# Two transformer blocks on one core: second-block attention with the values as stationary operand and strips turned two steps late; whole heads in the first block

## The chip, the cores and the metric

One core of a Trainium2 chip runs the whole program. The time is the device time of one execution in microseconds; what counts is the median over runs. TensorE (PE) multiplies, VectorE (DVE), ScalarE (ACT) and GpSimd (POOL) do elementwise work, and DMA queues issued by SyncE (SP) bring the weights.

## The reference

The input is 512 tokens of width 1024, in f32. Two blocks follow each other. In short:

```python
# block 1: proj = rmsnorm(x) @ w_in;  8 heads of width 64
logits = q @ k.T * scale + c_q - c_k          # c: cumulated log of a forget gate; causal
att = softmax(logits) @ v
sg  = u * (tril(w_s) @ rmsnorm(vg) + b_s)     # gated over chunks of 128 tokens, u, vg = gelu(...)
x  += concat(att, sg) @ w_out
x  += (silu(g) * a) @ w_down                  # a, g = split(conv3(rmsnorm(x) @ w_up)), 2816 wide
x   = rmsnorm(x)
# block 2: h = rmsnorm(x) * (1 + sc) + sh;  proj = h @ w_in_2
q, k, v = latent projections, rope on 32 of 96 columns     # "MLA", 8 heads, values 64 wide
o_mla = softmax(q @ k.T * scale, chunk-causal) @ v
o_ca  = softmax(cq @ ck.T * scale + rel_bias, chunk band) @ cv    # "chunk attention", 8 heads of 64
x += g_a * concat(o_mla, o_ca) @ w_out_2
x += g_m * conv_ffn(modulated rmsnorm(x))
```

## The kernel before

Activations lie as 128 partitions by columns. Large products are made exact enough by splitting both factors into a high and a low part and adding three products (hi by hi, hi by lo, lo by hi). `load_split` (L341 to L351) brings a weight by DMA into `wraw`, casts it to `whi` on ACT (L350) and subtracts to `wlo` on DVE or POOL (L351). The matrix product itself is one helper, so most TensorE rows carry its line, L372; the tiles' names tell them apart: `mm` are projections, `s` scores, `o` values.

TensorE takes its work in the order of the code. The other engines' work is ordered by a scheduler with priorities (`high_priority`), and each engine then works in order.

Both blocks' attention runs in `attention()` (L619 to L676), over a list of strips: a strip is 128 queries of one head against the `qi + 1` key blocks of 128 at or ahead of them (widths 128, 256, 384, 512). Step t does the following in this order:

- `strip_scores(t)`: the scores go into one bank of the pool `s` (three banks), DVE adds the bias or mask and keeps the minimum (L597), ACT takes the exponential into `p` and sums it (L601, with a read-accumulator instruction);
- background work `bg` (norms, rope), then half of the step's `fill` (projections and output products on TensorE, in amounts set by `rate(t)`);
- `strip_turn(t-1)`: the 128x128 blocks of `p` are transposed on TensorE (L610) back into the same `s` bank, which is copied to `pt` (L612) on whichever of ACT and DVE the scheduler chooses;
- the other half of `fill`, then `strip_values(t-2)`: per key block `pt` is the stationary operand (128x128) and `v` the moving one with 64 columns, f32; result `o` has queries on the partitions.

After the eight strips of a pair of heads, `pair_end` divides by the sums (L715, L717), transposes the result (L725) and splits it into `mix` for the output product. Heads prepare their operands in generators whose slices are taken ahead of need (`LEAD`, 5 steps). In block 1 `stack_k` casts and subtracts one half of `kh` and `kl` (L693, L694), and two DMAs on SP copy these to the other 64 partitions (L700).

In block 2 strips 0 to 31 (numbered within the block) are chunk attention, 32 to 63 are MLA. The q and k of a chunk-attention pair are transposed at L1633 after a norm (L1457); MLA's are transposed at L1667 and split into `hi`, `lo` (L1671 to L1675). Projections are evacuated from PSUM by `nc.any` (L1462, L1463, L1469, L1521, L1526, L1597). `final` (L942) scales the first block's result and is a background job; output part 0 needs it.

Of the kernel before, what the change touches and what calls it, by code (L numbers as in the profile page):

```python
# [19 lines left out]
P = 128  # L20
# [216 lines left out]
class Kernel:  # L237
# [99 lines left out]
    def load_split(self, src, pool, dest, skew):  # L337

        nc, n = self.nc, src.shape[-1]
        raw = self.wraw.tile([P, 1024], F32, tag="wraw", name="wraw")  # L340
        nc.sync.dma_start(out=raw[:, :n], in_=src)  # L341
        if dest:
            hi, lo = (self.pools[dest[0]].tile([P, 1024], F32R, tag=t, name="wsplit") for t in dest[1:])
        else:
            hi = self.whi.tile([P, 1088], F32R, tag="whi", name="whi")[:, skew:]
            lo = self.wlo.tile([P, 1088], F32R, tag="wlo", name="wlo")[:, skew:]
        with ExitStack() as ctx:
            for ins in self.before:
                ctx.enter_context(self.tc.issue_after(ins))
            nc.scalar.copy(hi[:, :n], raw[:, :n])  # L350
            (nc.gpsimd if pool else nc.vector).tensor_tensor(  # L351
                out=lo[:, :n], in0=raw[:, :n], in1=hi[:, :n].bitcast(F32), op=ALU.subtract)
        return hi, lo
# [264 lines left out]

    def attention(self, heads, fill, rate, bg, bgrate, mix, depth=1):  # L619

# [20 lines left out]
        for t in range(n + depth + 3):  # L641
            r = rate(t)
            if t < n:
                h, qi = seq[t]
                slices(h)
                sc[t] = self.strip_scores(hd[h], qi)
                for h in range(len(heads)):
# [5 lines left out]
            u = t - depth  # L653
            if 0 <= u < n:
                h, qi = seq[u]
                pt[u] = self.strip_turn(hd[h], qi, sc.pop(u))
            if t > n + depth:
                for f in later:
                    f()
                later = []  # L660
            fill.run(r / 2)
            for f in later:
                f()
            later = []
            u -= 1
            if 0 <= u < n:
                h, qi = seq[u]
                if u % 8 == 0:
                    o = self.bank("o")
                ov = 2 * qi + h % 2  # L670
                self.strip_values(hd[h], qi, pt.pop(u), o[:, ov * 64:(ov + 1) * 64])
                if h < last:
                    if u % 8 == 7:
                        later = [self.pair_end(o, mix, *hd[h]["end"])]
                elif u % 4 == 3:
                    later = [self.pair_end(o, mix, *hd[h]["end"], half=u % 8 // 4)]  # L676

# [11 lines left out]
    def stack_k(self, tiles, k, odd, scale=None):  # L689
        nc, (_, kh, kl) = self.nc, tiles  # L690
        a, b = HALF_P[::-1] if odd else HALF_P
        if scale is None:
            nc.scalar.copy(kh[a], k[a])  # L693
            nc.vector.tensor_tensor(out=kl[a], in0=k[a], in1=kh[a].bitcast(F32), op=ALU.subtract)  # L694
        else:
            nc.scalar.activation(out=kh[a], in_=k[a], func=AF.Copy, scale=scale[a])
            nc.vector.scalar_tensor_tensor(out=kl[a], in0=k[a], scalar=scale[a], in1=kh[a].bitcast(F32),
                                           op0=ALU.mult, op1=ALU.subtract)
        for t in (kh, kl):
# [9 lines left out]
    def pair_end(self, o, mix, sums, at, pool, tag, half=None):  # L709
# [12 lines left out]
        def turn():  # L722
# [6 lines left out]
            ins = self.split(mix[at], tp, c512)  # L729
            if half:  # L730

                self.before = ins
# [300 lines left out]
    def block1_mix(self, xn, x, evac, evac_last, norm_a):  # L1033
# [233 lines left out]
        def head(h):  # L1267
            fill.upto(f"qk{h // 2}") if h > 1 else None
            pr, odd = divmod(h, 2)
            sums, sh = self.sums(pairs, h)  # L1270

            cp = self.bank()
# [7 lines left out]
                in1=cmask.unsqueeze(1).to_broadcast([P, 4, P]), op=ALU.add)  # L1280
            yield
            tiles = self.stacked(stk)
            self.stack_q(tiles, qf[pr], odd)
            yield
            self.stack_k(tiles, kf[pr], odd)
            yield
            qs, kh, kl = tiles
# [8 lines left out]
            return dict(qk=[(qs, kh), (qs, kl)], bias=bias, v=lambda kb: vv[:, kb, h * 64:(h + 1) * 64], sums=sh,  # L1296
                        end=(sums, pr, mx, "mix"))

        cumulate()
        for _ in range(4):  # L1300
            fill.run(1500)
            bg.run(500)
        self.attention([head(h) for h in range(8)], fill, lambda t: 4500 if t < 0 else 3100, bg,
                       lambda t: 1300, mix)
        fill.drain()
# [55 lines left out]
    def block2_mix(self, xn, norm_b, final, evac, evac_last, norm_a):  # L1361
        nc, i = self.nc, self.i
        self.urgent = None
        ctx = ExitStack()
        self.pt = self.pool("pt2", 3, ctx=ctx)
        self.pp = self.pool("pp2", 3, ctx=ctx)
        self.att = self.pool("att2", 1, ctx=ctx)
        one = self.pools["one"] = self.pool("one2", 1, ctx=ctx)
        two = self.pool("two2", 2, ctx=ctx)
        stk = self.pool("stk2", 12, ctx=ctx)  # L1370
        tabq, tabk = tabs = [one.tile([P, 4, 4, 16], F32, name="tab" + z) for z in "qk"]
# [89 lines left out]
        def cq0_evac(t, ps):  # L1461
            nc.any.tensor_copy(out=ca_slice(t, 0, 0), in_=ps[:, 32:288])  # L1462
            nc.any.tensor_copy(out=kr[:, t], in_=ps[:, 0:32])  # L1463

        def ca_job(w, z, j, **kw):
            def dst(t):
                return vc[:, t, 256 * j:256 * (j + 1)] if z == 2 else ca_slice(t, z, j)

            yield from self.gemm_tm(i[w], 256, xn, lambda t, ps: nc.any.tensor_copy(out=dst(t), in_=ps), **kw)  # L1469
            if z < 2 and kw.get("pairs") != ((0, 1),):  # L1470
# [12 lines left out]
        def rope():  # L1483

            with self.tc.issue_after(self.applied):
                self.rope_tables(tabs)
            yield 6000

        def cq0():
            yield from self.gemm_tm(i["w_cq0"], 288, xn, cq0_evac)  # L1490
            bg.add("w_cq0", ca_norm(0, 0))
            bg.add("rope", rope())
            bg.add("final", final)

# [24 lines left out]
        def q_evac(c):  # L1519
            def f(t, ps):  # L1520
                nc.any.tensor_copy(out=mq[c][t // 2][:, t % 2], in_=ps.rearrange("p (h d) -> p h d", d=QK))  # L1521
            return f

        def k_evac(c):
            def f(t, ps):
                nc.any.tensor_copy(out=mk[c][t // 2][:, t % 2, :, 0:64],  # L1526
                                   in_=ps.rearrange("p (h d) -> p h d", d=64))
            return f
# [56 lines left out]
        def mla(c):  # L1585
            if c == 0:
                bg.add("kr", kr_rope())
            mq[c] = m_tiles(0, c)
            yield from self.gemm_tm(i[f"w_q{c}"], 384, [lath[0], lath[1]], q_evac(c))
# [6 lines left out]
            yield from self.gemm_tm(i[f"w_kv{c}"], 256, [lath[2]],  # L1596
                                    lambda t, ps: nc.any.tensor_copy(out=vm[c][:, t], in_=ps))  # L1597

# [57 lines left out]
        def mla_head(h):  # L1656
# [70 lines left out]
```

## Time and profile before

| what | us |
|---|---|
| median of 3 runs | 1227.69 (1226.39 to 1227.93) |
| profiled execution | 1225.62 |
| its span | 1223.9 |
| TensorE busy | 1193.0 |
| DVE busy | 780.2 |
| ACT busy | 526.5 |
| POOL busy | 190.5 |

The mean granted TensorE clock of the span is 0.997. TensorE's busy time is modelled at its ends, so a share of 97% doesn't say that it runs at its peak; what matters is where it sits idle, and which engine ends that. Block 1's mix stage lies at some 75 to 230 us, block 2's at some 575 to 880; the rest are the two feed-forward parts.

### The profile page before, as it was taken

The numbers are of one execution on the slowest core, as the hardware profiler recorded it, in microseconds if no ns is written. First come the engines' busy times: TensorE is split into PE (matmuls) and PEld (weight loads), VectorE is DVE, ScalarE is ACT, GpSimd is POOL, SyncE is SP. The second block draws the span as 40 slices with busy tenths as digits, with TensorE's granted clock in tenths as the row PEclk, the third lists the DMA queues.
The fourth block names the chain that finished last, engine by engine and source line by source line (L and its number), as shares of the span: only waits on it lengthen the run. The fifth ranks groups of instructions, "written<-read, shape, count | busy, mean of one in ns | idle before, by whom it ended". The sixth has DMA issues, their size and how long they took to land.

```text
span 1223.9 us, 17406 instructions
## 1 busy us (share of the span) xinstructions
PE 1193.0 (97%) x6730; PEld 1038.9 (85%) x6730; DVE 780.2 (64%) x1392; ACT 526.5 (43%) x946; POOL 190.5 (16%) x209
## 2 busy tenths in 40 slices
PE   9999898999999999999998989999999999999998
PEld 6898688988888888888998988899988888888887
DVE  6646777688888887433575878876675665653221
ACT  6535445454444443323434556655544444442110
POOL 2367301300000000000245472301200000000000
PEclk9999999999999999999999999999999999999999
DMA  7432222166666666433121333111133323233330
GB/s 237 120 102 78 82 82 61 53 188 196 200 192 190 193 190 190 144 98 128 58 86 57 87 109 104 36 36 36 53 123 102 103 86 104 93 89 112 114 110 18
DMA packets 42594, 135.78 MB, mean 111 GB/s; under 512 B 5120, under 2 KB 6016, under 8 KB 42512
## 3 DMA queue, kind: packets, MB, share of 16 engines
q1 hardware_dynamic: 34096, 106.84, 28.3%
q10 hardware_dynamic: 8208, 27.27, 7.4%
q8 instruction: 52, 0.85, 0.3%
q0 software_dynamic: 208, 0.57, 0.2%
q14 instruction: 30, 0.25, 0.1%
HBM read 128.37 MB, written 2.10 MB: 107 GB/s over the span
## 4 chain that ended last, share of the span: by engine, by line
PE 84%; DVE 6%; POOL 4%; issue 2%; ACT 2%; DMA 1%; SPq 0%; ACTq 0%; DVEq 0%; POOLq 0%
PE mm L372 74%; PE s L372 4%; PE o L372 3%; PE s L610 2%; POOL wlo L351 1%; ACT whi L350 1%; DVE wlo L351 1%; DVE s L597 1%; DVE ca L1457 1%; DMA x<-in_xT_dram 1%; POOL gelu L1111 0%; PE mm L1667 0%; DVE nt L557 0%; ACT p L601 0%; PE s L725 0%
## 5 line engine op out<-in xcount | busy, mean ns | idle before, releaser
L351 DVE TENSOR_TENSOR wlo<-wraw,whi 128x1024 fp32r<-128x1024 f32 (+4 forms) x182 | 210.3, 1157 | 180.6 <-ACT whi L350 179.5
L372 PE MATMUL mm<-xnh,whi 128*128 128x512 f32 (+1 forms) x832 | 310.8, 374 | 5.6 <-DVE x L877 2.7
L350 ACT CAST whi<-wraw 128x1024 fp32r<-128x1024 f32 (+4 forms) x194 | 191.6, 991 | 277.8 <-PE mm L372 260.2
L372 PE MATMUL mm<-xnl,whi 128*128 128x512 f32 (+1 forms) x832 | 309.7, 372 | 0.0
L372 PE MATMUL mm<-xnh,wlo 128*128 128x512 f32 (+1 forms) x832 | 309.7, 372 | 0.0
L372 PEld LDWEIGHTS mm<-xnh,whi 128*128 128x128 f32 x832 | 156.2, 188 | 33.5 <-DVE x L877 2.9
L372 PEld LDWEIGHTS mm<-xnh,wlo 128*128 128x128 f32 x832 | 156.1, 188 | 27.6
L372 PEld LDWEIGHTS mm<-xnl,whi 128*128 128x128 f32 x832 | 156.2, 188 | 26.7
L372 PE MATMUL mm<-gh,whi 128*128 128x512 f32 (+1 forms) x384 | 141.3, 368 | 1.1 <-DVE x L967 0.6
L372 PE MATMUL mm<-gh,wlo 128*128 128x512 f32 (+1 forms) x384 | 141.1, 367 | 0.0
L372 PE MATMUL mm<-gl,whi 128*128 128x512 f32 (+1 forms) x384 | 141.0, 367 | 0.0
L759 DVE SCALAR_TENSOR_TENSOR cv<-mm,cols,cv 128x510 f32<-128x510 f32 (+1 forms) x176 | 130.3, 745 | 2.5 <-ACT cv L757 0.5
L372 PE MATMUL mm<-whi,xnh 128*128 128x256 f32 (+3 forms) x304 | 96.5, 318 | 1.1 <-ACT xnh L842 1.1
L372 PE MATMUL mm<-wlo,xnh 128*128 128x256 f32 (+3 forms) x304 | 93.6, 308 | 0.2 <-DVE wlo L351 0.2
L372 PE MATMUL mm<-whi,xnl 128*128 128x256 f32 (+3 forms) x304 | 93.6, 308 | 0.1
L372 PEld LDWEIGHTS mm<-gh,whi 128*128 128x128 f32 x384 | 72.1, 188 | 13.5 <-DVE x L967 0.8
L372 PEld LDWEIGHTS mm<-gh,wlo 128*128 128x128 f32 x384 | 72.1, 188 | 12.1
L372 PEld LDWEIGHTS mm<-gl,whi 128*128 128x128 f32 x384 | 72.1, 188 | 12.0
L601 ACT ACTIVATE p<-s,st 128x128 f32<-128x128 f32 (+1 forms) x96 | 50.7, 528 | 70.4 <-DVE st L597 64.6
L1028 DVE CUSTOM_DVE_ANT_0 wada<-wada,cs,cols 128x1024 f32<-128x1024 f32 x48 | 61.5, 1282 | 28.9 <-DMA wada<-in_w_ada_dram 28.8
L372 PE MATMUL mm<-mix,whi 128*128 128x256 f32 (+1 forms) x288 | 73.8, 344 | 2.6 <-DVE x L877 1.5
L757 ACT ACTIVATE cv<-mm,cols 128x512 f32<-128x512 f32 x88 | 67.6, 773 | 0.0
(296 smaller groups left out, 1793.2 us busy)
## 6 DMA issues: line engine op xcount, KB each, us to landing
wraw<-in_w_up_dram SPq DMA_DIRECT2D x88, 512.0 KB, 3.6
wada<-in_w_ada_dram ACTq DMA_DIRECT2D x48, 512.0 KB, 3.7
wraw<-in_w_down_dram SPq DMA_DIRECT2D x32, 512.0 KB, 3.6
wraw<-in_w_out_dram SPq DMA_DIRECT2D x16, 512.0 KB, 3.7
wraw<-in_w_down_dram SPq DMA_DIRECT2D x16, 384.0 KB, 3.2
wraw<-in_w_qk_dram SPq DMA_DIRECT2D x8, 512.0 KB, 4.2
wraw<-in_w_v_dram SPq DMA_DIRECT2D x8, 256.0 KB, 4.9
x<-in_xT_dram SPq DMA_DIRECT2D x8, 256.0 KB, 6.5
```

Of the source, the lines that this page charges most:

```text
L350: nc.scalar.copy(hi[:, :n], raw[:, :n])
L351: (nc.gpsimd if pool else nc.vector).tensor_tensor(out=lo[:, :n], in0=raw[:, :n], in1=hi[:, :n].bitcast(F32), op=ALU.subtract)
L372: self.nc.tensor.matmul(out, lhsT, rhs, start=start, stop=stop, **kw)
L597: self.urgent = nc.vector.tensor_tensor_reduce(out=s[:, cs], in0=s[:, cs], in1=b, scale=1.0, scalar=3e38 if j == 0 else st[:, j - 1:j], op ...
L601: nc.scalar.activation(out=p[:, :nk], in_=s[:, :nk], func=AF.Exp, bias=st[:, len(parts) - 1:len(parts)], scale=-1.0, accum_out=hd["sums"](qi))
L610: self.nc.tensor.transpose(s[:, c], p[:, c], self.ident)
L757: nc.scalar.activation(out=t, in_=ps, func=AF.Identity, scale=w[2], bias=self.col(cb, n))
L759: nc.vector.scalar_tensor_tensor(out=t[:, d:], in0=ps[:, :512 - d], scalar=w[2 - d], in1=t[:, d:], op0=ALU.mult, op1=ALU.add)
L1028: nc.vector.tensor_tensor_reduce(out=w, in0=w, in1=self.cs, scale=1.0, scalar=self.col("b_ada_2", n), op0=ALU.mult, op1=ALU.add, accum_out ...
L1457: nc.vector.tensor_tensor(out=v3, in0=v3, op=ALU.mult, in1=ss[:, j, z, t].unsqueeze(2).to_broadcast([P, 4, 64]))
```

## The change

In block 2, `attention` is called with `depth=2, side=True`. A strip is now turned two steps behind its scores, by `side_turn` (transposes at L629, the copy always on ACT at L630 and into one tile for the head's four strips). After a pair's last strip `pair_values` multiplies for both heads with `v` (64 columns) as stationary operand and up to 512 columns of `pt` as moving one; the two heads alternate, one writing partitions 0 to 63 of `o`, the other 64 to 127. `side_end` no longer transposes `o` but the broadcast reciprocals of the sums (L793 on ACT, L799 on TensorE, L803 on ACT), and multiplies. There are four buffers for exponentials (`pp2`), two for turned heads, and nine for stacked operands. Evacuations go to ACT, `final` becomes a job of the second MLA part, and three pieces of fill (1500) with background work stand ahead of the loop. In block 1 a head is built in one piece two strips ahead (`ahead=2`) at high priority, and the second half of `kh` and `kl` is made by ACT and DVE in place of DMAs. POOL's share of `wlo` is cut in pieces of 256 columns.

```diff
@@ load_split
+            step = 256 if pool else n
+            for o in range(0, n, step):
+                c = slice(o, min(o + step, n))
+                (nc.gpsimd if pool else nc.vector).tensor_tensor(
+                    out=lo[:, c], in0=raw[:, c], in1=hi[:, c].bitcast(F32), op=ALU.subtract)
@@
+    def side_turn(self, pt, qi, sp):
+        nk = (qi + 1) * P
+        s, p = sp
+        for kb in range(qi + 1):
+            c = slice(kb * P, (kb + 1) * P)
+            self.nc.tensor.transpose(s[:, c], p[:, c], self.ident)
+        self.nc.scalar.copy(pt[:, qi:4 * qi + 1:3], s[:, :nk].rearrange("p (k q) -> p k q", q=P))
+
+    def pair_values(self, hds, pts, o, half=None):
+        q0, q1 = (0, 4) if half is None else (2 * half, 2 * half + 2)
+        for kb in range(q1):
+            a = max(q0, kb)
+            for z, (hd, pt) in enumerate(zip(hds, pts)):
+                p = pt.rearrange("p a b -> p (a b)")[:, (3 * kb + a) * P:(3 * kb + q1) * P]
+                self.mm(o[HALF_P[z], a * P:q1 * P], hd["v"](kb), p, kb == 0, kb == q1 - 1)
@@ attention, in step t
+            if ahead:
+                with self.tc.high_priority(offset=AHEAD):
+                    for h, _ in seq[:t + ahead + 1]:
+                        slices(h)
...
             fill.run(r / 2)
+            if side:
+                for f in later:
+                    f()
+                later = []
+                u = t - depth
+                w = u - 1
+                if 0 <= w < n and w % 8 == 7 or n - 8 <= w < n and w % 4 == 3:
...
+                    self.pair_values([hd[h - 1], hd[h]], [pt[h - 1], pt[h]], o, half)
+                    later = [self.side_end(o, mix, *hd[h]["end"], half=half)]
+                if 0 <= u < n:
...
+                    self.side_turn(pt[h], qi, sc.pop(u))
+                fill.run(r / 2)
@@ stack_k
         if scale is None:
-            nc.scalar.copy(kh[a], k[a])
-            nc.vector.tensor_tensor(out=kl[a], in0=k[a], in1=kh[a].bitcast(F32), op=ALU.subtract)
+            for o in (a, b):
+                nc.scalar.copy(kh[o], k[a])
+                nc.vector.tensor_tensor(out=kl[o], in0=k[a], in1=kh[a].bitcast(F32), op=ALU.subtract)
+            return
@@ side_end
+        nc.vector.reciprocal(sums[:, c8], sums[:, c8])
+        nc.scalar.copy(att[:, c512].rearrange("p (g d) -> p g d", d=64),
+                       sums[:, c8].unsqueeze(2).to_broadcast([P, 2 * len(qs), 64]))
+        def turn():
+            tp = self.bank()
...
+                nc.tensor.transpose(tp[:, t * P:(t + 1) * P], att[:, t * P:(t + 1) * P], self.ident)
...
+            nc.scalar.copy(att[:, c512], tp[:, c512])
+            nc.vector.tensor_tensor(out=att[:, c512], in0=o[:, c512], in1=att[:, c512], op=ALU.mult)
+            ins = self.split(mix[at], att, c512)
@@ block 2
-        self.pt = self.pool("pt2", 3, ctx=ctx)
-        self.pp = self.pool("pp2", 3, ctx=ctx)
+        self.pt = self.pool("pt2", 2, ctx=ctx)
+        self.pp = self.pool("pp2", 4, ctx=ctx)
-        stk = self.pool("stk2", 12, ctx=ctx)
+        stk = self.pool("stk2", 9, ctx=ctx)
-            nc.any.tensor_copy(out=ca_slice(t, 0, 0), in_=ps[:, 32:288])
+            nc.scalar.copy(ca_slice(t, 0, 0), ps[:, 32:288])
...
+        for _ in range(3):
+            fill.run(1500)
+            bg.run(800)
         self.attention(
             heads, fill,
-            lambda t: 3000 if t < 0 else 2000 if t < 16 else 1600 if t < 34 else 500,
-            bg, lambda t: 1700 if t < 16 else 600, mix)
+            lambda t: 1500 if t < 0 else 1900 if t < 16 else 1600 if t < 34 else 600,
+            bg, lambda t: 1700 if t < 34 else 1200, mix, depth=2, side=True)
```

On TensorE before, at two MLA strips in the second block (`s_7688` and `s_7715`; `s_7665` is the strip ahead of them), the order is scores, the turn of the strip ahead, projections, values:

```order
L372 MATMUL s_7688<-hi_7547,hi_7510 128x384 [waits PE_49]
L372 MATMUL s_7688<-lo_7548,hi_7510 128x384
L372 MATMUL s_7688<-hi_7547,lo_7511 128x384
L610 MATMUL s_7665<-ident_156,p_7671 128x128 [waits Activation_49]
L610 MATMUL s_7665<-ident_156,p_7671 128x128
L372 MATMUL mm_7701<-mix_7295,whi_7146 128x512 x2
L372 MATMUL mm_7701<-mix_7295,wlo_7147 128x512
L725 MATMUL s_7705<-ident_156,att_7686 128x128 [waits DVE_49]
L725 MATMUL s_7705<-ident_156,att_7686 128x128 x3
L372 MATMUL o_7713<-vm_6652,pt_7676 128x64 [waits PE_49]
L372 MATMUL s_7715<-hi_7547,hi_7510 128x512 [waits Activation_49]
```

On TensorE of the changed kernel at the same two strips (`s_7627`, then `s_7655`), with the values of a pair between them:

```order
L376 MATMUL mm_7636<-mix_7339,wlo_7126 128x512
L376 MATMUL o_7640<-pt_7465,vm_6595 64x512
L376 MATMUL o_7640<-pt_7559,vm_6595 64x512
L376 MATMUL o_7640<-pt_7465,vm_6595 64x384
L376 MATMUL o_7640<-pt_7559,vm_6595 64x384
L376 MATMUL o_7640<-pt_7465,vm_6595 64x256
L376 MATMUL o_7640<-pt_7559,vm_6595 64x256
L376 MATMUL o_7640<-pt_7465,vm_6595 64x128
L376 MATMUL o_7640<-pt_7559,vm_6595 64x128
L629 MATMUL s_7590<-ident_156,p_7596 128x128
L376 MATMUL s_7655<-hi_7522,hi_7482 128x512 [waits Activation_49]
```

The values moved from every step into one group per pair, and the turn is now that of the strip two steps back (`s_7590`), right ahead of the scores of the strip that uses its bank.

On ACT before, at the same place, exponentials (L601) and the copies of turned strips (L612); a copy follows the exponential of its own strip:

```order
L601 ACTIVATE p_7671,sums_7504<-s_7665,st_7669 128x256
L612 COPY pt_7698<-s_7665 128x256
L601 ACTIVATE p_7694,sums_7504<-s_7688,st_7692 128x384
L741 CAST mix_7710<-s_7705 128x512
L1671 CAST hi_7729<-mm_7724 96x512
L612 COPY pt_7736<-s_7688 128x384
L601 ACTIVATE p_7721,sums_7504<-s_7715,st_7719 128x512
```

On ACT of the changed kernel a few strips on (exponentials L605, copies L630):

```order
L605 ACTIVATE p_7695,sums_7476<-s_7689,st_7693 128x128
L630 COPY pt_7652<-s_7627 128x3x128
L605 ACTIVATE p_7727,sums_7476<-s_7721,st_7725 128x256
L630 COPY pt_7652<-s_7655 128x4x128
L605 ACTIVATE p_7743,sums_7476<-s_7737,st_7741 128x384
L630 COPY pt_7750<-s_7689 128x128
```

The copy of a strip (`s_7627`) now stands behind the exponential of the strip two later (`s_7689`), and the strip after that (`s_7721`) takes over its bank.

## Rows read from the trace of the kernel before

**Rows 1.** Page, part 1: busy time, share of the span, instructions.

```profile
PE 1193.0 (97%) x6730; PEld 1038.9 (85%) x6730; DVE 780.2 (64%) x1392; ACT 526.5 (43%) x946; POOL 190.5 (16%) x209
```

**Rows 2.** Windows: stretch, length; PE, PEld, DVE, ACT, POOL busy; clock; DMA share, GB/s.

```profile
659.30:662.70 3.40, 3.40 (x19) 3.40 (x18) 2.34 (x4) 1.80 (x4) 0.00 (x0) 0.50 0.11 33
664.40:767.10 102.70, 97.61 (x746) 92.75 (x744) 79.85 (x187) 58.49 (x148) 47.03 (x54) 1.00 0.33 92
767.10:832.00 64.90, 64.43 (x478) 59.26 (x478) 49.50 (x129) 40.34 (x109) 9.43 (x11) 1.00 0.10 34
```

**Rows 3.** Waits of TensorE, 570 to 890: total, times, longest.

```profile
PE mm L1633 <- DVE ca L1457: 3.4, 2, 2.2
PE mm L1633 <- DVE qs L687: 3.0, 2, 2.7
```

**Rows 4.** Waits of TensorE, 75 to 230.

```profile
PE mm L372 <- DVE mix L745: 2.8, 2, 2.6
PE mm L372 <- DVE kf L1186: 2.3, 1, 2.3
```

**Rows 5.** Timeline, TensorE, 654 to 665: start, length, instruction [idle before].

```profile
654.45 0.27 PE L1633 MATMUL mm<-ident,ca 128*128 128x128 f32 x1
...
658.45 1.21 PE L1633 MATMUL mm<-ident,ca 128*128 128x128 f32 x6 [2.17 <-DVE ca L1457]
659.31 0.56 PE L372 MATMUL mm<-whi,xnh 128*128 128x256 f32 x1
...
662.65 0.32 PE L372 MATMUL mm<-whi,xnh 128*128 128x256 f32 x1
...
664.42 0.28 PE L372 MATMUL s<-kh,qs 128*128 128x256 f32 x1
```

**Rows 6.** Timeline, MLA strips of the four widths, 783 to 794.

```profile
783.73 0.36 PE L372 MATMUL s<-hi 96*128 96x256 f32 x1
...
785.64 0.19 ACT L601 ACTIVATION_READ_ACCUMULATOR p<-s,st 128x1 f32 x1
...
786.32 0.36 PE L372 MATMUL s<-hi 96*128 96x256 f32 x1
...
787.58 1.00 PE L372 MATMUL o<-vm,pt 128*128 128x64 f32 x8
...
787.86 0.19 ACT L601 ACTIVATION_READ_ACCUMULATOR p<-s,st 128x1 f32 x1
788.38 0.42 PE L372 MATMUL s<-hi 96*128 96x384 f32 x1
...
789.47 0.37 ACT L612 COPY pt<-s 128x256 f32<-128x256 f32 x1 [1.42 <-PE s L610]
...
790.44 0.19 ACT L601 ACTIVATION_READ_ACCUMULATOR p<-s,st 128x1 f32 x1
790.50 0.47 PE L372 MATMUL s<-hi 96*128 96x512 f32 x1
...
792.40 0.36 PE L372 MATMUL s<-hi 96*128 96x256 f32 x1
...
793.35 0.20 ACT L601 ACTIVATION_READ_ACCUMULATOR p<-s,st 128x1 f32 x1
```

**Rows 7.** Source line L612, 575 to 878: ns min/median/max.

```profile
L612 ACT COPY pt<-s x51: 253/393/589, 669.1 to 835.4; 128x128 f32<-128x128 f32 x14, 128x512 f32<-128x512 f32 x14, 128x256 f32<-128x256 f32 x13, 128x384 f32<-128x384 f32 x10
```

**Rows 8.** Timeline, block 1: f32 products that stream 256 columns.

```profile
124.20 1.46 PE L372 MATMUL mm<-uv,wsp 128*128 128x256 f32 x6
...
125.49 0.49 PE L610 MATMUL s<-ident,p 128*128 128x128 f32 x3
```

**Rows 9.** Value records by form, chunk-attention and MLA stretch: busy, mean ns.

```profile
L372 PE MATMUL o<-vc,pt 128*128 128x64 f32 x146 | 19.6, 264 | 0.4 <-ACT pt L612 0.4
L372 PE MATMUL o<-vm,pt 128*128 128x64 f32 x138 | 18.6, 263 | 0.0
```

**Rows 10.** Block 1, 75 to 230, by form: the cast of k.

```profile
L693 ACT CAST kh<-kf 64x512 fp32r<-64x512 f32 x6 | 3.7, 615 | 0.0
```

More of the change, by code (lines that the diff above doesn't have):

```diff
@@ L617, in strip_values, with attention @@
             self.mm(o, pt[:, kb * P:(kb + 1) * P], hd["v"](kb), kb == 0, kb == qi)
-    def attention(self, heads, fill, rate, bg, bgrate, mix, depth=1):
+    def side_turn(self, pt, qi, sp):
[12 more added lines that the diff above has]
+                self.mm(o[HALF_P[z], a * P:q1 * P], hd["v"](kb), p, kb == 0, kb == q1 - 1)
+    def attention(self, heads, fill, rate, bg, bgrate, mix, ahead=None, depth=1, side=False):
         last = len(heads) - 2
@@ L646, in attention @@
                 sc[t] = self.strip_scores(hd[h], qi)
-                for h in range(len(heads)):
+                for h in range(len(heads)) if not ahead else ():
                     if 0 < seq.index((h, 0)) - t <= LEAD:
@@ L660, in attention @@
                 later = []
[L661 to L676, printed above, removed]
+                u = t - depth
@@ new lines, in attention @@
+                fill.run(r / 2)
+            else:
+                u = t - depth
+                if 0 <= u < n:
+                    h, qi = seq[u]
+                    pt[u] = self.strip_turn(hd[h], qi, sc.pop(u))
+                if t > n + depth:
+                    for f in later:
+                        f()
+                    later = []
+                fill.run(r / 2)
+                for f in later:
+                    f()
+                later = []
+                u -= 1
+                if 0 <= u < n:
+                    h, qi = seq[u]
+                    if u % 8 == 0:
+                        o = self.bank("o")
+                    ov = 2 * qi + h % 2
+                    self.strip_values(hd[h], qi, pt.pop(u), o[:, ov * 64:(ov + 1) * 64])
+                    if h < last:
+                        if u % 8 == 7:
+                            later = [self.pair_end(o, mix, *hd[h]["end"])]
+                    elif u % 4 == 3:
+                        later = [self.pair_end(o, mix, *hd[h]["end"], half=u % 8 // 4)]
@@ L1294, in bias @@
                 return r
-            return dict(qk=[(qs, kh), (qs, kl)], bias=bias, v=lambda kb: vv[:, kb, h * 64:(h + 1) * 64], sums=sh,
-                        end=(sums, pr, mx, "mix"))
+            return dict(qk=[(qs, kh), (qs, kl)], bias=bias, v=lambda kb: vv[:, kb, h * 64:(h + 1) * 64],
+                        sums=sh, end=(sums, pr, mx, "mix"))
+            yield
         cumulate()
@@ L1467, in dst @@
                 return vc[:, t, 256 * j:256 * (j + 1)] if z == 2 else ca_slice(t, z, j)
-            yield from self.gemm_tm(i[w], 256, xn, lambda t, ps: nc.any.tensor_copy(out=dst(t), in_=ps), **kw)
+            yield from self.gemm_tm(i[w], 256, xn, lambda t, ps: nc.scalar.copy(dst(t), ps), **kw)
             if z < 2 and kw.get("pairs") != ((0, 1),):
@@ L1520, in f @@
             def f(t, ps):
-                nc.any.tensor_copy(out=mq[c][t // 2][:, t % 2], in_=ps.rearrange("p (h d) -> p h d", d=QK))
+                nc.scalar.copy(mq[c][t // 2][:, t % 2], ps.rearrange("p (h d) -> p h d", d=QK))
             return f
@@ L1525, in f @@
             def f(t, ps):
[L1526 to L1527 removed]
+                nc.scalar.copy(mk[c][t // 2][:, t % 2, :, 0:64], ps.rearrange("p (h d) -> p h d", d=64))
             return f
@@ L1596, in mla @@
             yield from self.gemm_tm(i[f"w_kv{c}"], 256, [lath[2]],
-                                    lambda t, ps: nc.any.tensor_copy(out=vm[c][:, t], in_=ps))
+                                    lambda t, ps: nc.scalar.copy(vm[c][:, t], ps))
         def out0():
```

53 lines of the change are left out of this document (31 added, 22 removed).

## Prediction

> **What bounds the kernel now.** I read the page first: TensorE is busy 97% of the span [rows 1], so a gain must take work from it, or take one of its idle spells. Then the busy time by stage: in the second block's mix stage TensorE is busy 97.6 of the 102.7 us from the first chunk-attention score to the first MLA score, and 64.4 of 64.9 us from there to the last score, while ACT has 58.5 and 40.3 us of work and DVE 79.9 and 49.5 there [rows 2]. Then the table of waits: the longest ones of that stage are at L1633, the transposes of the chunk attention's q and k, which wait for their norm [rows 3]; in block 1 they are at a multiplication behind mix (2.6) and at projections behind `kf` (2.3) [rows 4]. Last the order of the work, since the change rewrites the strip loop: how long one strip takes from its scores to the end of its exponential, and which copy frees its score bank [rows 6].
>
> **Values, block 2.** Removed: 160 value records for chunk attention and 160 for MLA (146 and 138 of them lie in the two stretches [rows 9]). Eight records run from 787.58 to the next score at 788.38 [rows 6], 0.10 us each, so 32.0 us. Added: per head four products of 512, 384, 256 and 128 columns, 1280 together, two records each, since they are f32. The nearest f32 row streams 256 columns: six records from 124.20 to 125.49, 0.215 each [rows 8]. So 1280/256 x 2 x 0.215 = 2.15 us a head, 34.4 for 16 heads, if one head's product follows the other's. The two heads of a pair alternate, though, and each uses only half of the array's columns; if they stream side by side it is 17.2 us. No row of before shows two such products at once. I take side by side, as the heads write different halves of the bank and share no data, and keep the serial price as a rival.
>
> The Trainium skill has a rule on this, "TensorEngine Tiling (Array Packing)", Key Properties: tiles of the array run independently and in parallel. By it the sum is that of 17.2 us. The same section speaks against the change too: a change of tiling mode drains the engine, here at both ends of nine groups of values. It gives no price, and no row of before shows such a switch.
>
> **The first transposes and the clock.** From 654.45, where the first L1633 starts, to 659.31 there are 4.9 us, and the eight transposes need 0.9: 4.0 idle. Then the clock is granted at half (0.50 from 659.30 to 662.70 [rows 2]): 15 products from 659.31 to 662.65 take 0.223 each, the next 15 to 664.42 0.118 [rows 5], which is 1.6 us lost. In the changed order 138 products stand ahead of these transposes where 96 stood. These 42 x 0.118 = 5.0 us fill the gap, the clock has no idle spell ahead of it, and 5.6 us come back. By the first score 30 more products are done (3.5 us), which leave the stretch behind it. The first score comes 2.1 us earlier.
>
> **Chunk-attention stretch.** Work of 97.6 loses 3.5 (moved ahead) and 14.6 (146 records), and gains the values of six heads: 6.5 side by side, 12.9 serial. That is 86.0 or 92.4 us.
>
> **The new wait: a ring of three score banks.** Three banks hold the scores, so the scores of strip t need the copy of strip t-3 out of its bank. Before, that copy was done long ago: 789.47 to 789.84 for the scores at 792.40 or so, and the copy itself had waited for TensorE, not for ACT's queue [rows 6]. Now strips are turned two steps late. The copy of t-3 is issued in step t-1, directly ahead of SCORE(t), and in the order on ACT it stands behind the exponential of t-1 in nearly all steps of the first 20 strips and in 21 of the 31 steps between MLA scores. So SCORE(t-1), its bias on DVE, its exponential on ACT, the copy of t-3 and SCORE(t) form a chain, however much TensorE has to do. Its length per step: from a strip's first score product to the end of its read-accumulator 2.10 (783.73 to 785.83), 1.73, 2.25 and 3.05 us for the four widths [rows 6], 9.1 a head; the four copies 0.26 to 0.59, 1.7 together [rows 7]; 10.8 a head, 2.7 a step. In 3.05 ACT had another cast in front; without such delays the step is nearer 2.5. In bound steps TensorE has 60.0 us (below) / 31 = 1.9 on average to do, and 1.6 outside the four steps with values, so it waits about 1 us in each.
>
> MLA stretch: work 64.4, less 15.4 (138 + 16 records of the stretch), plus values of 8.6 heads (9.2 side by side, 18.5 serial), plus 12 output products of 256 columns that now lie ahead of the last score (1.4), plus 0.3 of transposes: 60.0 or 69.2. With the ring: 21 bound steps of 2.5 to 2.7 are 53 to 57, ten others at 1.9 are 19, and the four steps with values (2.15 in one step, and the transposes behind it) run past their chain by 1 us each: 76 to 80, I take 78, 13 more than 64.9. With serial values these four steps are 2.2 longer again, 87 in all, 22 more.
>
> Chunk stretch: TensorE has 2.6 a step there, on average as much as the chain needs, so only uneven steps lose. Bounds 0 and 11 us; I take 6 for the ring and what remains of the idle 5.1. That is 92 or 98.4 us against 102.7: -10.7 or -4.3.
>
> **ACT, DVE, pools.** Thirteen more evacuations, 13 more pt copies of 0.26 to 0.59 and nine copies of sums on ACT are some 15 us beside 98.8 in 167.6 us [rows 2]; the engine has room, and what it costs is the place in the queue, which the chain has in it. The two-buffered turned strips and the nine score operands bring no wait that I found ahead of the ring. The tail keeps its transposes and norm; 12 fewer output products (1.4) and shorter values make it -2 (serial -1).
>
> **Block 1.** Heads are built whole, two strips ahead, so the projections of a pair need not be drained at once; the 2.3 us behind `kf` [rows 4] go, the 2.6 behind mix stays. Sixteen transfers of k halves become eight casts of 0.62 [rows 10] and eight subtractions, about 5 us on ACT and 6 on DVE, neither full there but both ahead of exponentials, at high priority. Subtractions on POOL in four pieces may release weights earlier or cost issue time. I take -2, bounds -6 and +5.
>
> **Sum.** Against the profiled run, 1225.6 us: -2.1 - 10.7 + 13 - 2 - 2 = -3.8, 1221.8. The median of the three runs is 2.1 higher, so I forecast 1224 as a median. Own range 1215 to 1233, from the ring (8 to 11 us either way) and block 1.
>
> **Rivals.** *Serial values, on the slower side*: -2.1 - 4.3 + 22 - 1 - 2 = +12.6, a median of 1240. For it: the only f32 price measured is for one product after another, and every product has weights of its own to load. Against: the halves share nothing. It decides when the pair's eight products take 4.3 us rather than 2.2; already at 3.2 us the total is above before.
> *The ring costs nothing*, because ACT runs copies and exponentials early enough or TensorE's queued work covers the chain: -2.1 - 16.7 - 4.9 - 2 - 2 = -27.7, a median of 1200. For it: ACT is busy only 62% of the MLA stretch. Against: the chain is latency, not load, and the order puts the copy behind the exponential.
> *Serial values and no ring cost* (the change then does not bring what its swap of operands can): -2.1 - 10.3 + 4.3 - 1 - 2 = -11.1, a median of 1217.
> *The ring's waits lower the clock*: 4.0 us idle at 655 brought 0.50 for 3.4 us [rows 2, 5]; each such spell costs 1.6, six of them and the forecast's +13 becomes +23, 1233. Against: waits of 1 us are shorter than any that were followed by half clock in these rows.
>
> **How the numbers follow.** Forecast 0.42, serial 0.22, no ring 0.18, serial without ring 0.10, clock 0.08. What this kernel's measurement can tell from no change is about 0.2%, 2.5 us, that is 1225.2 to 1230.2. The forecast's own range puts 0.24 below, 0.10 inside and 0.08 above; serial 0.01, 0.02 and 0.19; no ring all below; serial without ring 0.09 below and 0.01 inside; clock 0.01, 0.02 and 0.05. Faster 0.53, same 0.15, slower 0.32. For 8 in 10 the range reaches from 1200, which leaves out half of the no-ring case, to 1243, above the serial case's centre.
>
> **What would show it.** In the changed trace: the eight value products of a pair in 2.2 or in 4.3 us; waits of TensorE's score products on ACT's copies, some 20 us in all, most of them between the MLA scores, 78 us from first to last; no wait at the first chunk transposes and a clock of 1.00 behind them; the first score 2 us earlier; the wait behind `kf` in block 1 gone. The forecast is wrong if MLA scores come every 2.0 us, if the clock falls there, or if block 1 moves by more than 6 us.

## The result, and the profile after

| | median us | runs | ratio to before |
|---|---|---|---|
| before | 1227.81 | 4 | |
| changed kernel | 1263.29 (1260.37 to 1265.69) | 4 | 1.029 (1.027 to 1.0309) |

The changed kernel is 35 us slower. The forecast was 1224, and the time lies 20 us above the wider range (1200 to 1243) and 30 above the forecast's own (1215 to 1233). Its profiled execution spans 1263.0 us, 39.1 more than before. Where the 39.1 lie follows from four dates in the trace: the end of block 1's feed-forward part, and the starts of the first chunk-attention score, of the first MLA score and of the last one:

| stretch | before | after | difference | forecast |
|---|---|---|---|---|
| start to the end of block 1's feed-forward part | 594.0 | 589.5 | -4.5 | -2 |
| from there to the first chunk-attention score | 70.4 | 71.7 | +1.3 | -2.1 |
| chunk attention, to the first MLA score | 102.7 | 122.9 | +20.2 | -10.7 |
| MLA, to the last score | 64.9 | 86.7 | +21.8 | +13 |
| to the end | 391.9 | 392.2 | +0.3 | -2 |

The page of the changed kernel, busy time by engine (answering to [rows 1]); TensorE has 9.1 us more busy time than before, although it has less to do; part of it is the lower clock shown below, at which a product takes longer:

```profile
PE 1202.1 (95%) x6546; PEld 1023.8 (81%) x6546; DVE 774.8 (61%) x1373; ACT 549.1 (43%) x999; POOL 199.6 (16%) x245
```

The table of waits of TensorE in the changed kernel's block 2 (total, times, longest; before: [rows 3]), from 570 to 920 us, then the same for the chunk stretch (661 to 784) and for the MLA stretch (784 to 871):

```profile
PE s L376 <- ACT pt L630: 35.0, 38, 7.1
PE s L376 <- DMA kh<-kh: 2.8, 1, 2.8
PE mm L376 <- ACT vm L1670: 1.8, 1, 1.8
...
PE s L376 <- DMA kl<-kl: 1.0, 1, 1.0
```

```profile
PE s L376 <- ACT pt L630: 19.0, 14, 7.1
```

```profile
PE s L376 <- ACT pt L630: 16.0, 24, 1.7
```

This one line is the ring: score products that wait for ACT's copy (L630) of a turned strip, 38 times and 35.0 us. Before, block 2's table has no line of scores that wait for a copy.

The stretches by window (columns as in [rows 2]): the chunk stretch and the MLA stretch of the changed kernel, then the time around the boundary between them:

```profile
661.20:784.10 122.90, 99.05 (x614) 84.57 (x614) 82.51 (x187) 66.40 (x167) 56.57 (x68) 0.90 0.28 83
784.10:870.80 86.70, 70.85 (x406) 50.86 (x406) 43.25 (x107) 46.12 (x123) 1.28 (x2) 0.93 0.05 17
```

```profile
764.00:772.00 8.00, 2.92 (x18) 2.21 (x16) 6.82 (x12) 4.23 (x9) 6.65 (x9) 1.00 0.19 67
772.00:796.00 24.00, 18.22 (x63) 11.82 (x63) 11.52 (x31) 10.38 (x29) 7.59 (x7) 0.50 0.13 45
796.00:800.00 4.00, 3.04 (x18) 2.36 (x19) 2.01 (x4) 2.18 (x6) 0.00 (x0) 1.00 0.00 0
```

Both stretches had a granted clock of 1.00 before and have 0.90 and 0.93 now. From 772 to 796 it is 0.50 (1.2 of 2.4 GHz) for 24 us on end; it fell during the wait of 7.10 us in the chunk stretch. Four shorter spells, near 664, 702, 726 and 746, came behind waits of 2.77, 3.20, 2.30 and 1.75 us. Here is the longest wait in the timeline (all engines; start, length, instruction, idle before):

```profile
764.74 0.39 PE L376 MATMUL s<-kl,qs 128*128 128x512 f32 x1
...
765.18 1.83 DVE L1621 TENSOR_TENSOR mqk<-mqk,nw 128x768 f32<-128x768 f32 x2 [2.29 <-POOL nw L530]
...
766.54 0.38 PE L629 MATMUL s<-ident,p 128*128 128x128 f32 x2
...
769.26 0.69 DVE L601 CUSTOM_DVE_ANT_0 s<-s,bs 128x512 f32<-128x512 f32 x1
...
772.92 0.69 ACT L605 ACTIVATE p<-s,st 128x512 f32<-128x512 f32 x1 [4.25 <-DVE nw L1607]
...
773.60 0.36 ACT L630 COPY pt<-s 128x256 f32<-128x256 f32 x1
774.02 0.58 PE L376 MATMUL s<-kh,qs 128*128 128x256 f32 x1 [7.10 <-ACT pt L630]
```

Read it upwards. The score at 774.02 waits for the copy at 773.60. That copy's own input, two transposes, was there from 766.9. It stands on ACT behind the exponential of the strip whose scores ended at about 765.1. That exponential ran only at 772.92, for two reasons. Its bias came at 769.26, behind a norm's multiplication, a weight's subtraction and rope work on DVE (the multiplication had itself stood 2.29 us at the head of DVE's queue, waiting for POOL). And then its buffer came free only after a sum of squares on DVE that ended near 772.9 (the squares of MLA's norms take buffers from the same pool as the exponentials). So here the delay of one strip on DVE and ACT stops TensorE.

The values of a pair, in an MLA step of the changed kernel, with the turn and the scores behind them:

```profile
814.16 2.38 PE L376 MATMUL o<-pt,vm 128*64 128x512 f32 x16
...
816.46 0.33 PE L629 MATMUL s<-ident,p 128*128 128x128 f32 x1
...
816.83 0.27 ACT L630 COPY pt<-s 128x128 f32<-128x128 f32 x1 [1.83 <-PE s L629]
817.15 0.50 PE L376 MATMUL s<-hi 96*128 96x512 f32 x1 [0.36 <-ACT pt L630]
```

Sixteen records, 2.30 us from the first to the next instruction, near the 2.15 that the prediction worked out for two heads streaming side by side.

### The profile page after: what moved, and what is told of

It reads as the page before. It is cut to its first block, busy times and chain, and to the rows that moved or that the text cites. A ratio compares the mean times of both kernels' runs of the same rounds, so it can differ in the third digit from the quotient of the medians.

```text
span 1263.0 us, 17042 instructions
## 1 busy us (share of the span) xinstructions
PE 1202.1 (95%) x6546; PEld 1023.8 (81%) x6546; DVE 774.8 (61%) x1373; ACT 549.1 (43%) x999; POOL 199.6 (16%) x245
## 5 line engine op out<-in xcount | busy, mean ns | idle before, releaser
L605 ACT ACTIVATE p<-s,st 128x128 f32<-128x128 f32 (+1 forms) x96 | 50.7, 528 | 68.7 <-DVE st L601 63.5
```

The costliest lines, as they stand in the source:

```text
L605: nc.scalar.activation(out=p[:, :nk], in_=s[:, :nk], func=AF.Exp, bias=st[:, len(parts) - 1:len(parts)], scale=-1.0, accum_out=hd["sums"](qi))
```

## The experiments

All ratios are to the kernel before, run with it on the same chip. The chips differ from group to group, and the kernel before took 1226.9 to 1229.2 us on them, so a difference of medians between two groups is uncertain by some 2 us; where it matters, the difference of the ratios is given beside it. The names of chunk and MLA stretch are those of the table above.

**The delay, taken out of the changed kernel.**

```diff
-            bg, lambda t: 1700 if t < 34 else 1200, mix, depth=2, side=True)
+            bg, lambda t: 1700 if t < 34 else 1200, mix, depth=1, side=True)
```

> The changed kernel with strips turned one step behind their scores in block 2 (depth=1), all else kept. Ring theory (SCORE(t) waits for the copy of strip t-3, which stands behind the exponential of t-1; in the changed kernel 35.0 us of waits, and clock granted below 1.00 behind them): the copy comes a step earlier, these waits fall under 6 us, the clock is 1.00 between the first and the last score, and the median falls to 1215 to 1228. Rival (the load that moved to ACT, or the exponentials that wait for shared p buffers, set the pace): waits stay over 20 us and the median stays over 1248.

Measured: 1238.35 us, ratio 1.008 (1.0061 to 1.01). The waits for copies fell from 35.0 to 4.5 us and the MLA stretch from 86.7 to 63.6, but the chunk stretch only from 122.9 to 118.2, with a clock of 0.88 where I expected 1.00. So the second step of delay costs 25 us here (26 by the ratios), nearly all of it between the MLA scores, and neither theory was the whole of it: 10 us above before remain. Waits of TensorE in this kernel, 655 to 880:

```profile
PE s L629 <- ACT p L605: 7.1, 9, 2.3
PE mm L1740 <- POOL sqm L1606: 5.3, 1, 5.3
PE s L376 <- ACT pt L630: 4.5, 2, 3.5
```

**The delay kept, a fourth score bank.**

```diff
-            self.open_psum(c3, mm=4, s=3, o=1)
+            self.open_psum(c3, mm=3, s=4, o=1)
```

> The changed kernel, still turned two steps late, with four score banks and three banks for projections in block 2 (before: three and four). Ring theory: SCORE(t) then waits for the copy of t-4, which was issued a step earlier, so the waits on copies fall under 8 us and the median to 1218 to 1235, a little above the kernel with depth 1 if three projection banks cost something. Rival (ACT's load or shared p buffers): no change, 1255 to 1265.

Measured: 1233.22 us, ratio 1.0037 (1.0024 to 1.005). The MLA stretch is 63.8 us, the chunk stretch 113.4, and the waits of scores for copies (655 to 880) have nearly gone:

```profile
PE s L376 <- ACT pt L630: 1.6, 2, 1.1
```

The ring theory holds: with one bank more (and one bank fewer for projections) the same two-step delay costs nothing between the MLA scores. What remains lies again in the chunk stretch.

**The delay alone, on the kernel before.**

```diff
-            bg, lambda t: 1700 if t < 16 else 600, mix)
+            bg, lambda t: 1700 if t < 16 else 600, mix, depth=2)
```

(and four buffers for exponentials, as in the changed kernel)

> The kernel before with nothing changed but the delay of the turn in block 2 (depth=2) and four buffers for exponentials; values, evacuations and rates as before. Ring theory: the delay alone brings the waits of score products on copies (20 to 40 us) and a clock under 1.00 behind them, median 1250 to 1275 (values on the path keep TensorE busier than in the changed kernel, so perhaps fewer waits). Rival (the delay is harmless, the loss comes with the swap of the operands and ACT's extra copies): 1222 to 1232.

Measured: 1259.18 us, ratio 1.0255 (1.0234 to 1.0275): chunk stretch 117.0 (102.7 before), MLA stretch 79.4 (64.9). The delay alone makes the kernel before 31 us slower, nearly as much as the whole change does. Its waits differ in one point that I had not expected:

```profile
PE s L372 <- DVE mix L742: 11.1, 7, 2.7
PE s L725 <- ACT pt L612: 5.3, 3, 3.3
...
PE s L372 <- ACT pt L612: 3.0, 6, 1.0
PE s L372 <- DVE pt L612: 2.8, 6, 1.0
```

Here the transposes at a pair's end (L725) take a score bank too, and with a ring of three that is the costliest tenant: 11.1 us of scores waiting for its split. The changed kernel put these transposes into a projection bank, so its ring has only the strips; here half of the delay's cost lies in the chunk stretch, in the changed kernel only 5 of 25.

**Block 1 alone.** Block 2 as before, block 1 and the weight split as in the change.

> Block 1 and the weight split as in the changed kernel, block 2 as before. The prediction's term for block 1 was -2 us (bounds -6 and +5): 1222 to 1233 with 1226 in the middle. In the changed kernel the wait behind kf is 1.5 where it was 2.3, waits of transposes on exponentials 2.9 where they were 2.0, so I expect within 2 us of before. Rival (block 1 carries a part of the loss): 1235 or more.

Measured: 1223.31 us, ratio 0.9959 (0.9943 to 0.9974). Block 1 brings 5 us, within the prediction's bounds but near their end, and more than the 2 that I expected before this run; 3.2 of them are there by the end of its feed-forward part. TensorE's waits of 75 to 230 us, against [rows 4]:

```profile
PE s L614 <- ACT p L605: 2.9, 3, 1.2
PE mm L376 <- DVE kf L1262: 1.5, 1, 1.5
PE mm L376 <- DVE mix L821: 1.0, 1, 1.0
```

**The swap of the operands alone**, on top of block 1's part; block 2's rates, evacuations and jobs as before.

```diff
-            bg, lambda t: 1700 if t < 16 else 600, mix)
+            bg, lambda t: 1700 if t < 16 else 600, mix, side=True)
```

(with two turned heads and nine stacked operands)

> Block 2 as before but for the swap of operands in the values (side=True with depth=1: two heads' values side by side, pt copies on ACT, sums copied by ACT) and the buffers that it needs (two turned heads, nine stacked operands); block 1 as in the changed kernel. Evacuations, rates, final and rope as before. The trace of the changed kernel shows 16 value records of a pair in 2.4 us where 160 records took 16 for eight heads, so the swap takes some 14 us of work off TensorE. Theory that the rest of the changed block 2 (rates, evacuations) costs what the ring does not: 1223.3 of e3_block1_only less 8 to 14, that is 1209 to 1216. Rival (the swap itself, by its bursts of values, its copies on ACT or fewer operand buffers, makes the waits of the chunk-attention stretch): 1225 to 1240.

Measured: 1223.82 us, ratio 0.9957 (0.9944 to 0.997): no difference from block 1 alone. The theory (1209 to 1216) is out; the rival was nearer, though its bounds were too high. The two stretches of block 1 alone, then of the swap (each second row ends some 0.5 us behind the start of the last score). With block 1 alone the chunk stretch is already 3.5 us longer than before, at a clock of 0.97, with two spells at half clock in it, near 663 and 707, where before the one spell lay ahead of it [rows 2]:

```profile
659.70:765.90 106.20, 100.59 (x744) 95.74 (x745) 79.41 (x187) 58.42 (x147) 47.78 (x60) 0.97 0.31 89
765.90:831.20 65.30, 64.82 (x480) 59.72 (x480) 50.03 (x130) 40.22 (x109) 9.43 (x11) 1.00 0.10 33
```

```profile
659.50:765.50 106.00, 92.29 (x646) 82.14 (x647) 77.39 (x186) 62.26 (x156) 47.75 (x58) 0.97 0.30 89
765.50:829.50 64.00, 61.35 (x402) 48.49 (x401) 45.15 (x120) 44.89 (x123) 12.62 (x14) 1.00 0.10 34
```

TensorE's busy time fell by 8.3 us in the chunk stretch, and the stretch by 0.2: the gain was turned into waits. They are these (655 to 880), where block 1 alone has 3.4 for `qs`, 1.6 for exponentials and none for `mqk`:

```profile
PE s L629 <- ACT p L605: 7.6, 9, 2.3
PE mm L1706 <- DVE qs L734: 5.2, 2, 4.4
PE mm L376 <- ACT mqk L1599: 2.8, 1, 2.8
```

**Evacuations.** The kernel of the first experiment with its evacuations on either engine.

```diff
-            nc.scalar.copy(ca_slice(t, 0, 0), ps[:, 32:288])
+            nc.any.tensor_copy(out=ca_slice(t, 0, 0), in_=ps[:, 32:288])
```

(and likewise the other five)

> e1_depth1 (1238) with the evacuations on either engine, as before. If the evacuations pinned to ACT set the chunk stretch of 118 us: down to 1222 to 1230. If background work on DVE ahead of the strips' bias does: little change, 1232 to 1242, or worse, since DVE gets some of them.

Measured: 1236.33 us, ratio 1.0059 (1.0041 to 1.0077), and a chunk stretch of 117.6. Pinning the evacuations to ACT is not what makes the chunk stretch long.

**Rates and the place of the background jobs.** The kernel of the first experiment with these, and the weight of rope among the background jobs (6000 in place of 3000), as before.

```diff
-            else:
-                bg.add("final", final)
...
+            bg.add("final", final)
...
-        for _ in range(3):
-            fill.run(1500)
-            bg.run(800)
...
-            lambda t: 1500 if t < 0 else 1900 if t < 16 else 1600 if t < 34 else 600,
-            bg, lambda t: 1700 if t < 34 else 1200, mix, depth=1, side=True)
+            lambda t: 3000 if t < 0 else 2000 if t < 16 else 1600 if t < 34 else 500,
+            bg, lambda t: 1700 if t < 16 else 600, mix, depth=1, side=True)
```

> e1_depth1 (1238) with the rates of fill and background work, rope's weight and the place of final as before, and without the three pieces ahead of the loop. In e1 the bias of a strip whose scores ended near 760.7 began on DVE at 768.99, behind rope and norm work. If the faster background rate (1700 up to step 34, 1200 later, against 1700 up to 16 and 600) is what fills DVE's queue: the chunk stretch falls from 118 to 95 to 105 and the median to 1212 to 1224. If the pinned evacuations do: 1232 to 1242.

Measured: 1222.18 us, ratio 0.9944 (0.993 to 0.9958), the shortest median of all. It is faster than the kernel before and the changed one, but its interval overlaps those of block 1 alone and of the swap alone. The chunk stretch is 102.2. So the schedule of fill and background work costs the other 16 us (17 by the ratios). The chunk stretch of the first experiment, then of this run:

```profile
662.30:780.50 118.20, 98.50 (x617) 86.72 (x617) 79.59 (x186) 65.23 (x166) 59.49 (x69) 0.88 0.30 85
659.50:761.70 102.20, 95.09 (x647) 84.37 (x647) 73.64 (x173) 65.56 (x168) 50.01 (x60) 0.96 0.31 92
```

The old schedule leaves 6.0 us less work on DVE and 9.5 less on POOL in this stretch. In the first experiment 7 of the 32 chunk strips had their bias on DVE start more than 3 us after their last score product, and here none had (2 in the kernel before). The clock has its part in the 16 us: a mean of 0.88 over 118.2 us is some 28 us at half clock, 0.96 over 102.2 us some 8 (taking the granted clock as either 0.50 or 1.00).

**Which part of the schedule.** Three kernels, each with one part of it put back in the kernel of the first experiment, and one that joins four banks with the old schedule and the two-step delay. The edit of the first is shown. The second puts back `final` and rope's weight, the third the fill with its three pieces, the last all of it together with `s=4` and `depth=2`.

```diff
-            bg, lambda t: 1700 if t < 34 else 1200, mix, depth=1, side=True)
+            bg, lambda t: 1700 if t < 16 else 600, mix, depth=1, side=True)
```

> e1_depth1 (1238) with only the rate of background work back (1700 up to step 16, then 600). If this rate puts norm and rope work ahead of the strips' bias on DVE, it alone gives most of the 16 us between e1 and f3: 1222 to 1229. If the place of final or the fill does, 1234 to 1242.

> e1_depth1 (1238) with only final and rope back (final among the first background jobs, rope weighed 6000). Late final stands behind the second MLA part, ahead of output part 0, which needs it at once, so its 16 products on DVE (0.47 each, 7.5 us) come in a burst between bias work there. If that burst makes the loss: 1222 to 1230. If the rate does: 1234 to 1242.

> e1_depth1 (1238) with only the fill back (no three pieces ahead of the loop, 3000 before the first strip, 2000, 1600, 500). Neither theory of the background work gives the fill more than a few us: 1233 to 1242. If it falls under 1230, the fill was what left TensorE without work in the chunk stretch.

> The changed kernel with its two-step delay kept, but with four score banks (three for projections) and the rates, rope's weight and place of final as before: e2_s4 (1233) and f3_rates_before (1222) in one. If the ring and the rates are separate causes that add, 1233 - 16 = 1217, range 1211 to 1222, faster than every kernel so far. If three projection banks or the delay itself cost something once the rates are mended, 1222 to 1228.

| kernel | median us | ratio | interval |
|---|---|---|---|
| background rate back | 1227.37 | 0.9997 | 0.9983 to 1.001 |
| `final` and rope back | 1229.01 | 1.0012 | 0.9997 to 1.0027 |
| fill back | 1233.11 | 1.0043 | 1.003 to 1.0057 |
| four banks, two-step delay, old schedule | 1223.34 | 0.9957 | 0.9943 to 0.9971 |

The background rate gives back 11 us, `final` with rope 9, the fill 5 (10, 8 and 5 by the ratios): more than 16 together, so what they relieve overlaps. My two theories were not alternatives. That the shared cause is the load in DVE's queue is argued, not shown: with only the rate put back, 7 chunk strips still have their bias more than 3 us late, as in the first experiment, although the kernel is 11 us faster. Four banks with the old schedule are no faster than three banks with a one-step delay, so the two-step delay brings nothing there; one projection bank fewer goes with it, and no run parts the two.

**Are the two halves really side by side?** The fastest kernel with a pair's values in another order.

```diff
-        for kb in range(q1):
-            a = max(q0, kb)
-            for z, (hd, pt) in enumerate(zip(hds, pts)):
+        for z, (hd, pt) in enumerate(zip(hds, pts)):
+            for kb in range(q1):
+                a = max(q0, kb)
```

> f3_rates_before (1222) with a pair's values in another order: all products of one head, then all of the other, so that consecutive products write the same half of the columns. If the two halves stream side by side only when the two heads alternate: a pair's 16 records take 4.3 us instead of 2.4, TensorE has 16 us more to do, and the median rises to 1228 to 1240, most of it between the MLA scores, where TensorE hardly waits. If the order doesn't matter (the records would be cheap for another reason): 2.4 us a pair, 1219 to 1225.

Measured: 1233.61 us, ratio 1.006 (1.0044 to 1.0077), 11 us more than with alternation (14 by the ratios; the chips differ). Eight pairs at 1.56 us more each are 12.5. Of the 9.1 us between the two profiled spans 4.3 lie between the MLA scores and 3.0 in the chunk stretch, so "most of it" there was too much. In this kernel's timeline:

```profile
785.47 3.93 PE L376 MATMUL o<-pt,vm 128*64 128x512 f32 x16
789.33 0.33 PE L629 MATMUL s<-ident,p 128*128 128x128 f32 x1
```

3.86 us to the next instruction instead of 2.30. The two heads' products overlap when they alternate and hardly at all in this order; this was the step on which the forecast and its serial rival parted, and here the forecast was right.

## Why the prediction was wrong

**Where the miss lies.** The runs take the change apart step by step, and the steps add up to the measured loss. Their prices are differences of ratios, in us of 1228; the forecast's are the terms of its sum.

| step | forecast | measured |
|---|---|---|
| block 1 | -2 | -5 |
| swap of the operands (work and idle time taken off TensorE in block 2) | -20.1 | 0 |
| evacuations to ACT, a fourth buffer for exponentials | 0 | -2 (not clear of noise) |
| schedule: fill ahead of the loop, rates, `final`, rope | -5.6 | +17 |
| second step of delay with three score banks | +24 | +26 |
| sum | -4 | +36 |

The -20.1 are 8.1 us of work and 5.1 of idle time in the chunk stretch, 4.9 of work in the MLA stretch and 2 behind it; the -5.6 are the 2.1 and the 3.5 of the first transposes; the +24 are 6 in the chunk and 18 in the MLA stretch. Each price holds at its place in this order; on the kernel before, the delay alone costs 31.

**The step that failed: work taken from TensorE was counted as time.** The forecast took "Work of 97.6 loses 3.5 (moved ahead) and 14.6 (146 records), and gains the values of six heads", made 86.0 us of it, and let the chunk stretch be as long as that work and 6 us more, because TensorE was busy 97.6 of 102.7 us there [rows 2]. In the swap alone TensorE had 8.3 us less to do in the chunk stretch, and the stretch was 0.2 us shorter; between the MLA scores 60.0 was worked out and no run with the swap and the old schedule came under 62. The no-ring rival, formed in the same way, gave 1200; the runs without ring waits and with the old schedule stand at 1222 to 1224, of which block 1 is 5. What showed up in place of the gain are waits for exponentials, for `qs` and for an evacuation, most of which TensorE had not had to wait for before.

**A term with the wrong sign: the schedule of fill and background work.** The three pieces of fill ahead of the loop had a term of -5.6 (the transposes' gap filled). The new rates, the place of `final` and rope's weight, all part of the change, had none. Together they cost 17 us (the step from the old schedule to the first experiment). In the kernel of the first experiment one strip's scores were out at 760.7, and its bias ran at 768.99:

```profile
760.40 0.34 PE L376 MATMUL s<-kl,qs 128*128 128x384 f32 x1
...
762.32 1.83 DVE L1621 TENSOR_TENSOR mqk<-mqk,nw 128x768 f32<-128x768 f32 x2 [2.79 <-POOL nw L530]
...
768.33 0.74 DVE L1030 SCALAR_TENSOR_TENSOR x<-mm,mod,x 128x512 f32<-128x512 f32 x1
...
768.99 0.55 DVE L601 CUSTOM_DVE_ANT_0 s<-s,bs 128x384 f32<-128x384 f32 x1
```

The multiplication at 762.32 had waited for POOL at the head of DVE's queue for 2.79 us, and rope work, a sum of squares and an output came behind it, all ahead of the bias.

**The ring: right mechanism, right size in sum.** Both the trace (35.0 us of waits for copies) and the runs (25 us between two-step and one-step delay, nothing with a fourth bank between the MLA scores) show it. Between the MLA scores the forecast had 18 us of it; the stretch is 23 longer than with one step of delay (86.7 against 63.6), with waits of 16.0 and 12 us at half clock among them. In the chunk stretch it had 6, from bounds of 0 and 11; the waits there are 19.0, but where only 4.5 or 1.6 of them are left the stretch is just 5 or 9 us shorter (118.2 with one step of delay, 113.4 with a fourth bank): other waits, 7.1 and 5.3 in the first experiment, have taken their place. So a wait's length in the table is not what removing it brings. The forecast's "most of them between the MLA scores" did not hold of the waits, 16.0 of 35.0, though it holds of the cost.

**The clock.** I gave it a chance of 0.08 and a price of 10 us, on the ground that the ring's waits of 1 us are too short. It did fall, behind single waits that I had not foreseen (7.10, 3.20 and 2.30 for copies, 2.77 for a transfer). In the 24 us at 0.50 TensorE was busy 18.2; at full clock that would be about 9, which bounds what this spell cost, as part of it was bound by the chain anyway. What the clock alone costs was not separated by a run.

**Values: right.** A pair side by side was worked out as 2.15 us, and 2.30 was measured; the serial 4.3 came out as 3.86. The rule of the Trainium skill, "TensorEngine Tiling (Array Packing)", Key Properties, that tiles run independently and in parallel, agrees with the 2.30. No row here prices its other rule there, a drain at each change of mode; if the worked-out 2.15 is right, two changes fit into the 0.15 us between.

**The first transposes.** Their wait went as forecast: the eight run at 655.37 without a stall. What the forecast didn't ask is what is late next. It is the transfer of the other half of `kh`, for which the first score waits 2.8 us, and 1.0 for `kl`, where 4.0 of idle time stood before:

```profile
655.37 1.04 PE L1706 MATMUL mm<-ident,ca 128*128 128x128 f32 x8
...
661.23 0.36 PE L376 MATMUL s<-kh,qs 128*128 128x256 f32 x1 [2.77 <-DMA kh<-kh]
```

Behind it the clock fell for a spell near 664, where the forecast had 1.00, so the 1.6 us of the clock did not come back either.

**Block 1** was -2 and is -5 alone. The wait behind `kf` was to go and fell only from 2.3 to 1.5; the one behind mix was to stay and fell from 2.8 to 1.0. What the rest of the 5 us is was not looked for.

**The chances.** Slower had 0.32, more than half of it for serial values, which did not happen; the slowdown came from elsewhere.

What stays open: how much of the chunk stretch's loss is clock and how much is waiting; what a two-step delay with three banks costs under the old schedule once the values are swapped; and whether buffers for the squares apart from those for exponentials would shorten the waits that remain. None of these was tried.

## What to carry to other kernels

Before delaying a step by one more iteration, count the buffers that the delayed step keeps occupied: a ring of three that just covered a delay of one turns a delay of two into a chain through every engine, and one more buffer undoes it. A schedule of background work is a term of its own: what it puts at the head of an in-order queue, such as an instruction that waits there for another engine, delays what the critical loop has behind it. And work taken from an engine that is busy 95% of a stretch is a gain only until the next engine is late, which the table of waits shows only once the first has got out of the way. The same holds of waits: those for copies in the chunk stretch fell from 19.0 us to 4.5 or 1.6, and the stretch by 5 or 9.

## What the runs showed of the hardware

Products that each use 64 of the 128 columns overlap nearly fully when they alternate between the halves, 2.30 us for 16 records where 2.15 was worked out for full overlap, and hardly at all when the same half follows itself, 3.86 us where 4.3 was worked out for none. After one idle spell of 7.10 us the clock stayed at 0.50 for more than 20 us in a stretch where TensorE kept waiting, while before, with the queue full behind it, an idle spell of 4.0 us was followed by 3.4 us at 0.50 [rows 2, 5].
